# The MLP's first product as seven block products for eight, with weight sums made by adding DMAs

## The chip, the cores and the metric

The kernel runs on one core of a Trainium2 chip. The metric is the device time of one execution in microseconds (us), taken as the median of several runs. One execution of the kernel before was also recorded by the profiler; all rows below are from that one. The engines are called TensorE (PE in the rows; PEld is its weight loading), VectorE (DVE), ScalarE (ACT), GpSimd (POOL) and SyncE (SP).

## What is computed

One layer on a sequence of 512 tokens of width 1024, in float32: a mixer of two branches (retention with 8 heads, and sparse attention with 16), merged by gates; then an MLP; then a gated input from a per-layer embedding; then a last norm. The MLP is the part that the change rewrites:

```
h2 = rms_norm(x, norm_mlp_g)
x = x + square(relu(h2 @ w_mlp_up)) @ w_mlp_down
x = x + (p @ w_ple_proj) * sigmoid(rms_norm(x, norm_ple_g) @ w_ple_gate)
return rms_norm(x, norm_final_g)
```

`w_mlp_up` is 1024 x 4096 and `w_mlp_down` 4096 x 1024. In the retention, every head's output goes through a group norm, `(o - mean) * rsqrt(var + eps)`, over its 256 columns.

## The kernel before

Every product is made of three matmuls in a rounded float32 format: both operands are split into a high part (ScalarE's copy, `hi`) and a low part (VectorE's subtraction, `lo`), and `mm3` adds high by high, low by high and high by low in one PSUM bank. So each weight that comes from memory costs one pass of ScalarE and one of VectorE before TensorE can use it. Activations lie transposed (128 features by 512 tokens), so that a weight block of 128 by 128 is loaded into TensorE and 512 token columns stream past it. The retention's value product and the last product stream 256 columns past a loaded block in places.

The program is a list of items in one order, written by hand. An item has a TensorE part, a step after it (`post`) and the weight parts (512 columns each) that it needs. `run` goes through the list: it splits the item's own parts if they aren't, records its matmuls, splits up to three parts ahead (the fourth one's high part too), records what earlier items deferred, and then the item's `post`. Each engine works through its own instructions strictly in that order. A weight piece (1024 columns, 512 KB) is loaded by a DMA that SyncE issues as soon as one of three buffers (`raw`) is free, that is, when VectorE has made the low part of the second half of the piece three before it; high and low parts have four buffers each.

The stages that matter here: the retention's heads (`head_dense` of head h interleaved with `head_core` of head h-1, about 40 us a head, and after every second head `ret_out`, about 22 us); the attention; the merge and `w_out`, which makes the residual `x1` in eight blocks of 128 features; the MLP in two halves of 2048 hidden units, each `up` (16 products of 24 matmuls) and then `down` (8 products of 48); the embedding's gate product and the delivery of the output.

Around the changed lines: `gained` makes the high and low part of a block of `x1` (`gx`) and adds its squares to `acc1`. `token_rstd` and `over_partitions` make the token norm's factor `rb1`, by which `up`'s step multiplies. `rsqrt` is nine small instructions, on VectorE or, for heads 0 to 6 (`pool if h < NH - 1 else dve`) and for the first two token tiles of the output, on GpSimd. `gated` is the step that makes a head's output ready for `ret_out`. `finish` and `deliver` are the steps of the output's four token tiles; the last tile's second half is computed in two products of 256 columns.

Of the kernel before, what the change touches and what calls it, by code (L numbers as in the profile page):

```python
# [140 lines left out]
def _layer_kernel(ctx, tc, a, out):  # L141
# [35 lines left out]
    def issue(p):  # L177
        if p.keep:
            if p.raw is None:
                p.raw = P_[p.keep].tile([P, p.n], F32, name=f"raw_{p.keep}_{p.mark}")  # L180
                sp.dma_start(p.raw, p.src)
        elif p.raw is None:
# [3 lines left out]
            sp.dma_start(p.raw, p.src)  # L186
# [607 lines left out]
    def head_core(h):  # L794
# [36 lines left out]
        def post():  # L831
# [9 lines left out]
            rs = rsqrt(ve, NQ, "gn", pool if h < NH - 1 else dve)  # L841
# [29 lines left out]
        its.append(Item(0.9, turn, gated))  # L871
# [40 lines left out]
    items += [sil0, g0[0], b0[1], g0[1], c1[3], g0[2], c0[0], g0[3], c1[4], c0[1], qk0[0], c0[2], qk0[1], c0[3], qk0[2], qk0[3], c0[4]]  # L912
    for h in range(1, NH):
        its = mixed(head_dense(h), head_core(h - 1))
# [334 lines left out]
    def merge_start():  # L1249
        close("aw", "q", "kv")  # L1250
        T["nsa_p"] = []
        open_("np", bufs=1)
        open_("mp", bufs=1, side="right")
# [42 lines left out]
    def out_start():  # L1296
        close("mw", "np", "oret")
        xp = open_("xp", bufs=1)
        T["x1"] = [xp.tile([P, S], F32, name=f"x1_{n}") for n in range(KT)]
        T["gx"] = [(xp.tile([P, S], F32R, name=f"gx_hi{n}"), xp.tile([P, S], F32R, name=f"gx_lo{n}")) for n in range(KT)]  # L1300
        T["rb1"] = xp.tile([P, S], F32, name="rb1")
        open_("ew", bufs=2)
# [3 lines left out]
    def gained(n, g, acc):  # L1306

        hi, lo = T["gx"][n]
        x = T["x1"][n]
        gc = gains[:, g + n : g + n + 1]  # L1310
        act.activation(hi, x, AF.Copy, scale=gc)
        dve.scalar_tensor_tensor(lo, x, gc, hi.bitcast(F32), op0=ALU.mult, op1=ALU.subtract)
# [8 lines left out]
    for n in range(KT):  # L1321
# [5 lines left out]
        def post_x(ps, n=n):  # L1327
            dve.tensor_tensor(T["x1"][n], ps, T["xs", n], op=ALU.add)
            gained(n, G_MLP, "acc1")
# [4 lines left out]
    gxs = (lambda: T["gx"], KT)  # L1334
    hid = {}

    def up(hf, i):
        def post(ps):
            t = P_["ew"].tile([P, S], F32, tag="t1", name="relu")
# [289 lines left out]
```

## Time and profile before

| | |
|---|---|
| median of 3 runs | 1269.36 us (1267.52 to 1271.04) |
| the profiled execution's own time | 1269.14 us |
| its span in the trace | 1267.4 us |
| mean granted TensorE clock | 0.997 of full speed |
| TensorE busy | 1245.6 us, 98% of the span |
| VectorE, ScalarE, GpSimd busy | 61%, 42%, 17% |

The profile is read from the busy shares to the waits of the engine that is busy all the time, and from there to single stretches: what a matmul takes there from start to start, and what the other engines have to do in the same stretch. A duration of a row can overlap the next row's by the pipeline of an engine, so spacing is read from starts.

### The profile page before, as it was taken

The page shows a single profiled execution, that of the slowest core. Times are in us where ns is not written, and L with a number is a line of the kernel's source. Part 1 is how long each engine was busy: PE and PEld are TensorE (multiplying, and loading weights), DVE is VectorE, ACT ScalarE, POOL GpSimd, SP SyncE. Part 2 cuts the span into 40 slices and gives each one's busy share as a digit, 9 for nine tenths or more (in the row PEclk, how much of TensorE's full clock was granted, in tenths as well). Part 3 has the DMA queues.
Part 4 walks back from the last instruction along what each step waited for, and adds up shares of the span by engine and source line. Part 5 has one row for each costly group of instructions (what it writes and reads, how often), then busy time and mean ns, then how long its engine had stood idle before and what let it go on. Part 6 is the DMA issues. An engine that isn't in the chain of part 4 may idle for free.

```text
span 1267.4 us, 16784 instructions
## 1 busy us (share of the span) xinstructions
PE 1245.6 (98%) x6312; PEld 1033.0 (82%) x6312; DVE 770.9 (61%) x1401; ACT 528.8 (42%) x1091; POOL 213.4 (17%) x290
## 2 busy tenths in 40 slices
PE   8999999999999999999999999999999999999996
PEld 6968898898998987788888888888888888888885
DVE  6766763665666587778878754555652345644456
ACT  5753333332332233677778642343322223323333
POOL 0040000000000023556574500000000000000045
PEclk9999999999999999999999999999999999999998
DMA  7532323223223222211010033332233342323221
GB/s 248 204 133 67 105 79 100 76 92 100 76 78 98 86 73 84 67 34 35 34 51 17 18 100 100 122 127 91 93 100 100 98 168 86 98 100 100 88 79 67
DMA packets 34513, 116.29 MB, mean 92 GB/s; under 512 B 4096, under 2 KB 4480, under 8 KB 34304
## 3 DMA queue, kind: packets, MB, share of 16 engines
q1 hardware_dynamic: 34432, 115.22, 27.8%
q8 instruction: 50, 0.82, 0.3%
q14 instruction: 31, 0.25, 0.1%
HBM read 111.01 MB, written 4.19 MB: 91 GB/s over the span
## 4 chain that ended last, share of the span: by engine, by line
PE 50%; DVE 2%; POOL 0%; ACT 0%; issue 0%; DVEq 0%; ACTq 0%
PE ps_s L256 6%; PE ps_s L257 6%; PE ps_s L258 6%; PE ps_d L256 4%; PE ps_d L258 4%; PE ps_d L257 4%; PE ps_v L256 3%; PE ps_v L257 3%; PE ps_v L258 3%; PE ps_t L1089 2%; PE ps_t L258 1%; PE ps_t L257 1%; PE ps_t L256 1%; PE ps_v L1106 1%; PE ps_v L1105 1%; PE ps_s L1014 1%
## 5 line engine op out<-in xcount | busy, mean ns | idle before, releaser
L206 ACT ACTIVATE hi<-raw 128x512 fp32r<-128x512 f32 (+1 forms) x364 | 222.7, 622 | 256.4 <-PE ps_v L258 60.5
L209 DVE TENSOR_TENSOR lo<-raw,hi 128x512 fp32r<-128x512 f32 (+1 forms) x350 | 242.5, 715 | 67.7 <-ACT hi L206 67.6
L209 POOL TENSOR_TENSOR lo_fw<-raw_fw,hi_fw 128x512 fp32r<-128x512 f32 x8 | 11.3, 1437 | 503.0 <-ACT hi_fw L206 503.0
L256 PE MATMUL ps_d<-h_hi,hi 128*128 128x512 f32 x216 | 89.6, 415 | 0.0
L258 PE MATMUL ps_d<-h_hi,lo 128*128 128x512 f32 x216 | 85.4, 395 | 0.0
L257 PE MATMUL ps_d<-h_lo,hi 128*128 128x512 f32 x216 | 85.3, 395 | 0.0
L1067 POOL TENSOR_TENSOR pr<-pr,rr 128x512 f32<-128x512 f32 x80 | 84.5, 1087 | 0.0
L1032 ACT ACTIVATE pr<-ps_s,nm 128x128 f32<-128x128 f32 (+3 forms) x128 | 66.0, 525 | 21.5 <-DVE sc L1026 15.5
L256 PE MATMUL ps_t<-h_hi,hi 128*128 128x512 f32 x160 | 64.2, 401 | 0.0
L1098 DVE TENSOR_TENSOR ptl<-ps_t,pth 128x512 fp32r<-128x512 f32 x80 | 53.9, 684 | 16.5 <-ACT pth L1093 14.5
L258 PE MATMUL ps_t<-h_hi,lo 128*128 128x512 f32 x160 | 63.4, 396 | 0.3 <-DVE lo L209 0.3
L257 PE MATMUL ps_t<-h_lo,hi 128*128 128x512 f32 x160 | 63.3, 395 | 0.0
L1024 DVE TENSOR_REDUCE nm<-ps_s 128x2 f32<-128x256 f32 (+3 forms) x64 | 52.1, 815 | 14.3 <-PE ps_s L1017 14.0
L302 POOL TENSOR_TENSOR rs_q<-rs_y 128x4 f32<-128x4 f32 (+1 forms) x9 | 4.4, 491 | 325.9 <-DVE rs_y L292 325.9
L1343 ACT ACTIVATE hh<-relu 128x512 fp32r<-128x512 f32 x32 | 20.3, 634 | 93.5 <-DVE relu L1340 93.5
L1093 ACT ACTIVATE pth<-ps_t 128x512 fp32r<-128x512 f32 x80 | 47.3, 598 | 22.6 <-PE ps_t L1089 18.6
L258 PE MATMUL ps_s<-hh,lo 128*128 128x512 f32 x128 | 50.8, 397 | 0.0
L256 PE MATMUL ps_s<-hh,hi 128*128 128x512 f32 x128 | 50.7, 396 | 0.0
L257 PE MATMUL ps_s<-hl,hi 128*128 128x512 f32 x128 | 50.7, 396 | 0.0
L256 PE MATMUL ps_s<-gx_hi,hi 128*128 128x512 f32 x128 | 50.6, 395 | 0.0
L258 PE MATMUL ps_s<-gx_hi,lo 128*128 128x512 f32 x128 | 50.5, 395 | 0.0
L257 PE MATMUL ps_s<-gx_lo,hi 128*128 128x512 f32 x128 | 50.5, 395 | 0.0
(459 smaller groups left out, 3388.4 us busy)
## 6 DMA issues: line engine op xcount, KB each, us to landing
raw<-in_w_ret_qkg_dram SPq DMA_DIRECT2D x32, 512.0 KB, 3.4
raw<-in_w_mlp_up_dram SPq DMA_DIRECT2D x32, 512.0 KB, 3.7
raw<-in_w_mlp_down_dram SPq DMA_DIRECT2D x32, 512.0 KB, 3.6
raw<-in_w_ret_v_dram SPq DMA_DIRECT2D x16, 512.0 KB, 3.5
raw<-in_w_ret_o_dram SPq DMA_DIRECT2D x16, 512.0 KB, 3.5
raw<-in_w_merge_gate_dram SPq DMA_DIRECT2D x16, 512.0 KB, 3.6
raw<-in_w_nsa_dram SPq DMA_DIRECT2D x12, 512.0 KB, 3.5
o_ret<-in_cmp_w_dram SPq DMA_DIRECT2D x8, 512.0 KB, 5.1
```

What stands on the lines that cost most here:

```text
L206: act.activation(p.hi[i], p.raw[:, c], AF.Copy)
L209: eng.tensor_tensor(p.lo[i], p.raw[:, c], p.hi[i].bitcast(F32), op=ALU.subtract)
L256: pe.matmul(ps, sh, mh, start=first, stop=False)
L257: pe.matmul(ps, sh, ml, start=False, stop=False)
L258: pe.matmul(ps, sl, mh, start=False, stop=last)
L1024: dve.tensor_reduce(self.nm[:, j, :], self.seen(j), axis=AX.XY, op=ALU.max, negate=True)
L1032: act.activation(self.pr[:, j, br, 0 : self.nk].rearrange("p (b j) -> p b j", j=P), self.seen(j)[:, br], AF.Exp, bias=self.nm[:, j, br : b ...
L1067: pool.tensor_tensor(p, p, self.rr[:, :, 1 + br : 2 + br].broadcast_to([P, 4, P]), op=ALU.mult)
L1089: pe.transpose(self.t[i][:, j * P : (j + 1) * P], self.pr[:, j, br, kb * P : (kb + 1) * P], ident)
L1093: act.activation(hi, self.t[i], AF.Copy)
L1098: dve.tensor_tensor(lo, self.t[i], self.pt[i][0].bitcast(F32), op=ALU.subtract)
L1343: act.activation(hi, t, AF.Square)
```

## The change

**The product.** Per pair q of output blocks (16 pairs) the weights are four blocks `w[i][j]` (i: which 512 input features, j: which 128 outputs) and the activations four blocks (512 features by 256 tokens). Where eight products of blocks did the work, seven do now, on sums and differences of blocks (the scheme of Strassen and Winograd). Four of the seven use a sum of weights, `s1` to `s4`; all stream 256 token columns. Partial results are taken out of PSUM in between, since three banks per pair are each used for more than one of the products. The token factor is no longer multiplied into `up`'s result; its square (`rb2`) is multiplied into `down`'s.

**The weight sums** are made in device memory by 32 plain copies that ScalarE issues and 32 adding DMAs that GpSimd issues, 512 KB each, spread by `among` over heads 1 to 6. MLP weights then come in 56 pieces of two DMAs of 256 KB each, where they came in 32 pieces of 512 KB.

**The activations' sums** (`combined`, in `w_out`'s stage): VectorE makes the difference `t1` and GpSimd three more, each of 128 by 256.

**Around it.** `rsqrt` is on VectorE everywhere; the last head's `gated` is recorded ahead of the splits; `w_out`'s step defers `gained`; the output's steps come in another order, the last product's gain is multiplied on VectorE, and ScalarE issues one of the last two stores.

```diff
@@ Piece
+    def load(self, sp):
+        if isinstance(self.src, list):
+            for i, x in enumerate(self.src):
+                w = self.n // len(self.src)
+                sp.dma_start(self.raw[:, i * w : (i + 1) * w], x)
...
@@ _layer_kernel
+    w_up = a["w_mlp_up"].rearrange("(q i) k (j c) -> i j q k c", i=2, j=2)
+    sums = {x: dram.tile([16, P, S], F32, name=f"sum_{x}") for x in ("s1", "s2", "s3", "s4")}
+    def sum_steps():
+        todo = {}
+        for c in range(8):
+            q = slice(2 * c, 2 * c + 2)
+            w = lambda i, j, q=q: w_up[i, j, q]
+            t = {x: v[q] for x, v in sums.items()}
+            levels = [("s1", w(1, 1)), ("s3", w(0, 0)), ("s2", w(0, 0)), ("s4", w(0, 1))], [("s1", w(1, 0)), ("s3", w(1, 0))], [("s2", t["s1"])], [("s4", t["s2"])]
+            for l, level in enumerate(levels):
+                todo.setdefault(c + l, []).extend((t[x].rearrange("q k c -> k q c"), src.rearrange("q k c -> k q c"), l > 0) for x, src in level)
+        return [lambda d=d, s_=s_, add_=add_: pool.dma_start(d, s_, accum_op=ALU.add, max_dma_last_dim=4 * S) if add_ else act.dma_start(d, s_) for n in sorted(todo) for d, s_, add_ in todo[n]]
...
-            rs = rsqrt(ve, NQ, "gn", pool if h < NH - 1 else dve)
+            rs = rsqrt(ve, NQ, "gn")
...
-        its.append(Item(0.9, turn, gated))
+        its.append(Item(0.9, turn, gated, eager=h == NH - 1))
...
     for h in range(1, NH):
-        its = mixed(head_dense(h), head_core(h - 1))
+        its = among(mixed(head_dense(h), head_core(h - 1)), folds_[64 * (h - 1) // 6 : 64 * h // 6])
...
+    def combined(n, g):
...
+        taken("x10", k, t[:, :H])
+        taken("x11", k, t[:, H:])
+        pool.tensor_tensor(d, d, t[:, H:], op=ALU.add)
+        pool.tensor_tensor(t0[:, H:], t[:, H:], t0[:, H:], op=ALU.subtract)
+        pool.tensor_tensor(t0[:, :H], d, t[:, :H], op=ALU.subtract)
+        def rest():
+            taken("t2", k, d, -1.0)
+            taken("t3", k, t0[:, H:])
+            taken("t4", k, t0[:, :H])
+        defer(rest)
...
             dve.tensor_tensor(T["x1"][n], ps, T["xs", n], op=ALU.add)
-            gained(n, G_MLP, "acc1")
+            defer(lambda: gained(n, G_MLP, "acc1", True))
...
+    class UpPair:
+        def product(self, name, piece, col):
+            ps_, x, first = {"p5": ("b", "t1", True), "m1": ("a", "x00", True), "m2": ("c", "x10", True), "p6": ("a", "t2", False), "p3": ("b", "x11", False),
+                             "p7": ("a", "t3", False), "p4": ("a", "t4", False)}[name]
+            def go():
+                if first:
+                    tag = {"a": "dv"[self.q % 2], "b": "t", "c": "s"}[ps_]
+                    setattr(self, ps_, bank(tag, (P, H)))
+                ps = getattr(self, ps_)
+                for k in range(4):
+                    mm3(ps, *piece.cols(col + k * P, col + k * P + P), *seventh(x, k), first and k == 0, k == 3, not first)
...
+        def squares(self, i, t):
...
+            dve.scalar_tensor_tensor(t, t, 0.0, t, op0=ALU.min if i else ALU.max, op1=ALU.mult)
+            act.activation(hi, t, AF.Copy)
+            defer(lambda: dve.tensor_tensor(lo, t, hi.bitcast(F32), op=ALU.subtract))
...
+        order_ = [("p5", 0), ("m1", 0), ("p5", 1), ("m1", 1), ("m2", 0)]
+        for i in range(6):
+            order_ += [("p6", i)] + [("m1", i + 1)] * (i > 0) + [("p3", i), ("p7", i), ("p5", i + 2), ("m2", i + 1), ("p4", i)]
...
     def down(hf, n):
-            dve.tensor_tensor(x, ps, x, op=ALU.add)
+            t = P_["ew"].tile([P, S], F32, tag="t1", name="dn")
+            dve.tensor_tensor(t, ps, T["rb2"], op=ALU.mult)
+            dve.tensor_tensor(x, x, t, op=ALU.add)
...
-            st["r"] = rsqrt(v, 1, "fn", pool if t < NQ - 2 else dve)
+            st["r"] = rsqrt(v, 1, "fn")
...
+            behind.extend([gate_, *scaled, held, take, square] if t == NQ - 1 else [gate_, take, *scaled, square])
```

On ScalarE, in the middle of head 1 (`th`, `inh`, `vh` and `rth` are steps of the head, `hi` a weight's high part), the order before is:

```order
L206 ACTIVATE hi<-raw 128x512 x2
L754 ACTIVATE th<-ps_v 128x512
L316 ACTIVATE inh<-inn 128x256
L316 ACTIVATE inh<-inn 128x128
L206 ACTIVATE hi<-raw 128x512 x4
L764 ACTIVATE vh<-ps_d 128x512
L764 ACTIVATE vh<-ps_v 128x512
L867 ACTIVATE rth<-gated 128x512 x2
```

and after it is as follows, with the copies of weight sums (`sum_s`) among the same instructions:

```order
L214 ACTIVATE hi<-raw 128x512 x2
L780 ACTIVATE th<-ps_v 128x512
L360 DMA sum_s_81<-in_w_mlp_up_dram 128x2x512
L324 ACTIVATE inh<-inn 128x256
L324 ACTIVATE inh<-inn 128x128
L360 DMA sum_s_83<-in_w_mlp_up_dram 128x2x512
L214 ACTIVATE hi<-raw 128x512 x4
L790 ACTIVATE vh<-ps_d 128x512
L790 ACTIVATE vh<-ps_v 128x512
L360 DMA sum_s_80<-in_w_mlp_up_dram 128x2x512
L893 ACTIVATE rth<-gated 128x512 x2
```

Nothing else moved there: five or six copies a head stand between the head's own steps.

On VectorE, in the middle of `up`, two output blocks of the kernel before (`relu` is the step's result, `hl` its low part, `lo` a weight's low part) are:

```order
L1340 SCALAR_TENSOR_TENSOR relu<-ps_s,rb_8181 128x512
L1344 TENSOR_TENSOR relu<-relu 128x512
L1345 TENSOR_TENSOR hl<-relu,hh 128x512
L209 TENSOR_TENSOR lo<-raw,hi 128x512 x2
L1340 SCALAR_TENSOR_TENSOR relu<-ps_d,rb_8181 128x512
L1344 TENSOR_TENSOR relu<-relu 128x512
L1345 TENSOR_TENSOR hl<-relu,hh 128x512
L209 TENSOR_TENSOR lo<-raw,hi 128x512 x2
```

and one pair (seven products) after it is, from the step after `m2` to the next pair's (`r` are the two results of a pair, `s` the partial results that ScalarE took out of PSUM):

```order
L1467 TENSOR_TENSOR r_9209<-ps_s,s_9125 128x256
L217 TENSOR_TENSOR lo<-raw,hi 128x512
L1481 COPY r_9168<-ps_d 128x256
L1489 SCALAR_TENSOR_TENSOR r_9168<-r_9168 128x512
L217 TENSOR_TENSOR lo<-raw,hi 128x512
L1491 TENSOR_TENSOR hl<-r_9168,hh 128x512
L217 TENSOR_TENSOR lo<-raw,hi 128x512 x2
L1473 TENSOR_TENSOR r_9209<-ps_t,s_9125 128x256
L1489 SCALAR_TENSOR_TENSOR r_9209<-r_9209 128x512
L217 TENSOR_TENSOR lo<-raw,hi 128x512
L1491 TENSOR_TENSOR hl<-r_9209,hh 128x512
L1478 TENSOR_TENSOR r_9313<-ps_v,s_9036 128x256
```

With the two `lo` that follow, a pair has seven low parts of weights where it had four, four steps of 256 columns that read PSUM, and two squares with their low parts.

## Rows read from the trace of the kernel before

**Rows 1.** The page: busy time and share by engine; tenths in 40 slices.
```profile
PE 1245.6 (98%) x6312; PEld 1033.0 (82%) x6312; DVE 770.9 (61%) x1401; ACT 528.8 (42%) x1091; POOL 213.4 (17%) x290
PEclk9999999999999999999999999999999999999998
```
**Rows 2.** Waits of TensorE: line, waited for, us in total, times, longest.
```profile
PE ps_d L256 <- ACT hi L206: 5.8, 1, 5.8
PE ps_d L257 <- DVE rtl L868: 1.0, 2, 0.7
PE ps_d L256 <- ACT rth L867: 0.3, 1, 0.3
```
**Rows 3.** Timeline of TensorE (start, duration): first matmuls of second `up`, second `down`.
```profile
1026.87 0.39 PE L256 MATMUL ps_d<-gx_hi,hi 128*128 128x512 f32 x1
...
1116.47 0.40 PE L256 MATMUL ps_d<-hh,hi 128*128 128x512 f32 x1
```
**Rows 4.** Stretches: us, busy (x) of PE, PEld, DVE, ACT, POOL, clock, DMA share, GB/s.
```profile
95.00:390.00 295.00, 295.00 (x1690) 257.35 (x1689) 180.97 (x350) 97.32 (x180) 15.71 (x66) 1.00 0.28 86
1027.00:1116.00 89.00, 89.00 (x383) 71.58 (x382) 51.06 (x78) 27.94 (x47) 0.00 (x0) 1.00 0.32 111
1249.94:1255.55 5.61, 5.61 (x49) 5.60 (x47) 4.26 (x11) 2.99 (x7) 4.09 (x10) 1.00 0.26 96
```
**Rows 5.** Timeline of TensorE's weight loading in `up`.
```profile
929.93 0.19 PEld L257 LDWEIGHTS ps_s<-gx_lo,hi 128*128 128x128 f32 x1
```
**Rows 6.** Timeline of VectorE in the first `up`.
```profile
900.79 1.28 DVE L209 TENSOR_TENSOR lo<-raw,hi 128x512 fp32r<-128x512 f32 x2
903.64 0.69 DVE L1340 SCALAR_TENSOR_TENSOR relu<-ps_v,rb 128x512 f32<-128x512 f32 x1 [1.56 <-PE ps_v L258]
905.03 0.69 DVE L1344 TENSOR_TENSOR relu<-relu 128x512 f32<-128x512 f32 x1 [0.70 <-ACT hh L1343]
905.75 0.69 DVE L1345 TENSOR_TENSOR hl<-relu,hh 128x512 fp32r<-128x512 f32 x1
```
**Rows 7.** Groups by line and form: busy us, mean ns of one.
```profile
L814 DVE TENSOR_TENSOR inn<-ps_t,dec 128x256 f32<-128x256 f32 x8 | 3.3, 417 | 0.0
L537 ACT ACTIVATE vcat<-ps_v 128x256 fp32r<-128x256 f32 x1 | 0.4, 385 | 0.0
L206 ACT ACTIVATE hi<-raw 128x512 fp32r<-128x512 f32 x356 | 219.5, 626 | 256.4 <-PE ps_v L258 60.5 <-PE ps_d L257 53.4 <-PE ps_s L257 52.9
L1432 POOL TENSOR_TENSOR x2t<-x2t,gf 128x256 f32<-128x256 f32 x2 | 1.8, 902 | 0.0
```
**Rows 8.** DMA queue (packets, MB, share of 16 engines); issues (KB each, us to landing).
```profile
q1 hardware_dynamic: 34432, 115.22, 27.8%
raw<-in_w_mlp_up_dram SPq DMA_DIRECT2D x32, 512.0 KB, 3.7
xs<-in_xT_dram SPq DMA_DIRECT2D x8, 256.0 KB, 4.0
```
**Rows 9.** Timeline of the issuing queue in the heads: one issue, one decay table.
```profile
230.31 0.33 SPq L186 DMA_DIRECT2D raw<-in_w_ret_qkg_dram  x1
230.69 0.42 SPq L781 DMA_DIRECT2D dec<-in_decay_dram  x1
```
**Rows 10.** VectorE's wait for the group norm's factors: us, times, longest.
```profile
DVE on L846 <- POOL rs_y L298: 21.0, 7, 3.0
```
**Rows 11.** Timeline at the end: GpSimd beside VectorE, last matmul, last scaling.
```profile
1245.92 1.29 POOL L1432 TENSOR_TENSOR x2t<-x2t,gf 128x512 f32<-128x512 f32 x1 [3.61 <-ACT sq L1431]
1245.99 1.77 DVE L1427 TENSOR_TENSOR x2t<-x2t,pth 128x512 f32<-128x512 f32 x1
1255.48 0.28 PE L258 MATMUL ps_s<-hi_fw,gx_lo 128*128 128x256 f32 x1
1260.38 0.14 DVE L1443 TENSOR_SCALAR fv<-ss 128x1 f32<-128x1 f32 x1
1263.08 0.72 ACT L1451 ACTIVATE o<-x2t,rs_y 128x512 f32<-128x512 f32 x1 [3.22 <-DVE rs_y L300]
```

More of the change, by code (lines that the diff above doesn't have):

```diff
@@ L1313, in gained @@
+    def gained(n, g, acc, seven=False):
+        x = T["x1"][n]
+        if seven:
+            combined(n, g)
+        else:
+            hi, lo = T["gx"][n]
+            gc = gains[:, g + n : g + n + 1]
+            act.activation(hi, x, AF.Copy, scale=gc)
+            dve.scalar_tensor_tensor(lo, x, gc, hi.bitcast(F32), op0=ALU.mult, op1=ALU.subtract)
         if n == 0:
@@ L1390, in ple_start @@
+    dn = [down(1, n) for n in range(KT)]
+    items += dn[0] + [Item(0, load_pp)] + sum(dn[1:], [])
     def ple_start():
         close("hid")
-        open_("fw", bufs=1, side="right")
+        open_("fw", bufs=1)
         for p in w_pg[1]:
@@ L1482, in _layer_kernel @@
     items += weave(first[16:], turns[4:])
-    behind, late, last = [], [], [(), ()]
-    def finished(steps, ends=(), turn=True):
-        gate_, take, square = steps
-        behind.extend([gate_, *late[:1], take, *(last.pop(0) if turn else ()), *late[1:]])
-        late[:] = [square, *ends[:1]]
-        last.append(ends[1:])
+    behind = []
+    f_ = [finish(t, 0, S, lambda t=t: pw[0, t], 0) for t in range(NQ)]
+    behind.append(f_[0][0])
     for t in range(NQ):
-        finished(finish(t, 0, S, lambda t=t: pw[0, t], 0))
+        behind.extend([*(f_[t + 1][:1] if t + 1 < NQ else ()), *f_[t][1:]])
     banks = iter("ttdvs")
+    scaled = []
     for t in range(NQ):
@@ L1510, in _layer_kernel @@
                         add(Item(0, None, behind.pop(0)))
-            ends = deliver(t, 2 + (t == NQ - 1)) if c1 == S else ()
-            finished(finish(t, S + c0, S + c1, lambda t=t, c0=c0, n=c1 - c0: pw[1, t, c0][:, :n], 1 + (c0 > 0)), ends, t < NQ - 1 or c0 > 0)
-    items += [Item(0, None, f) for f in [*behind, late[0], *last[0], late[1], *last[2]]]
+            gate_, take, square = finish(t, S + c0, S + c1, lambda t=t, c0=c0, n=c1 - c0: pw[1, t, c0][:, :n], 1 + (c0 > 0), c0 == 0)
+            if t == NQ - 1 and c0 == 0:
+                behind.extend([gate_, take])
+                held = square
+                continue
+            behind.extend([gate_, *scaled, held, take, square] if t == NQ - 1 else [gate_, take, *scaled, square])
+            factors, last_ = deliver(t, 2 + (t == NQ - 1))
+            behind.append(factors)
+            scaled = [last_]
+    items += [Item(0, None, f) for f in [*behind, *scaled]]
     run(items)
```

198 lines of the change are left out of this document (138 added, 60 removed).

## The prediction, made before the changed kernel ran

> **What bounds the kernel now.** I read the busy shares first: TensorE works 1245.6 of 1267.4 us and no other engine passes 61%, at the full granted clock in every slice but the last [rows 1]. The waits of TensorE come next: of its 21.8 us without work, 5.8 are the first weights at the start, about 1.3 are waits for a head's output (`rth`, `rtl`) [rows 2], and 11.9 lie behind the last matmul, which starts at 1255.48 [rows 11]. So time goes away only with TensorE's work, its few waits, or the tail. The second `up` shows it at its plainest: 384 matmuls of 512 columns from 1026.87 to 1116.47 [rows 3], 0.2333 us from start to start, TensorE busy for 89.00 of 89 us [rows 4]. The sum is made against the profiled execution's own time, 1269.14 us: its span of 1267.4 and 1.7 around it. That is the median of the runs shown (1269.36) to 0.02%.
>
> **The product.** Out go 2 x 384 = 768 matmuls at 0.2333: 179.2 us. In come 16 pairs x 7 products x 4 blocks x 3 = 1344 matmuls of 256 columns. Their price stands in the last stretch of the trace, where 48 matmuls of this form take 5.61 us [rows 4]: 0.1169 each, half of the wide ones to within 0.2%. 1344 x 0.1169 = 157.1 us. **Saved: 22.1 us**, if TensorE is fed.
>
> One thing speaks against that half. In the 256-column stretch weight loading is busy for 5.60 of 5.61 us, in `up` for 71.58 of 89 [rows 4]; there is no room left behind the matmuls for a slower load. The Trainium skill (TensorE: Matmul & The Clock Gate, Back-to-back issue gap) has the spacing set by the load and the matmul together, 81 ns at 128 columns and 131 at 512, so that half the columns are not half the time: about 0.75 of it at 256, my estimate on a straight line between its figures, by which the product would cost 235 us and the sum below would end 78 us higher, near 1326. The measured half decides.
>
> **Feeding it.** A pair takes TensorE 84 x 0.1169 = 9.8 us. VectorE has seven `lo`, two squares, two `hl` and four steps of 256 columns in that time. Two 512-wide instructions that don't need each other start 0.60 apart (a pair of 0.69 takes 1.28); one that needs the one before starts 0.72 after it [rows 6]; a 256-wide one takes 0.42 [rows 7]. 11 x 0.60 + 4 x 0.42 = 8.3 us, 85%. I walked one period in the order that stands in the code, from the end of `p4`: copy and square done at 1.3, `lo`, `hl` (its high part comes back from ScalarE 1.4 after the square's start, as from 903.64 to 905.03 in rows 6) at 2.7, two `lo` at 3.9, then a wait for `p3` (4.2), two more steps, `lo`, `hl` at 6.9, the step after `p7` at 7.2, two `lo` at 8.4, the step after `m2` at 9.0, `lo` at 9.6, and a wait for the next `p4`. Each `lo` is there 2 to 3 us ahead of its product, and each bank is empty before its next use. ScalarE has 7 x 0.63 + 3 x 0.39 + 2 x 0.63 = 6.8 us. Loads: two of 256 KB every 2.8 us, 187 GB/s; the queue moved 115.22 MB in 27.8% of the span, so at full work about 327 GB/s, and a 256 KB load lands in 4.0 us [rows 8]. A buffer comes free two pieces (5.6 us) before VectorE wants the new data; issue 0.33 [rows 9], landing 4.0 and ScalarE's 0.63 leave 0.6, and then the 2 to 3 us above. So nothing waits in the steady part. Both halves begin and end less evenly (`p4` of the last pair comes one product behind `p7`, whose step waits behind a `lo` and an `hl`): I take **+1.5** for both, between 0 and 13 (the rival below).
>
> **The sums of weights.** 64 DMAs of 512 KB are spread over six stretches of 40 us, 10.7 in each, beside loads that take 0.28 of the DMA engines [rows 4], or 11 us. No row shows a copy from memory to memory or an adding one. At 327 GB/s a copy is 1.6 us of all engines and an add lies between 1.6 and 4.8 (three passes): 17 to 34 us, in all 28 to 45 of 40. I take two passes for an add, 36 of 40. A load is needed every 5.6 us with a cover of two pieces less its landing of 3.7 [rows 8], 11.2 - 3.7 = 7.5 us; if three queues share the engines evenly, 1.6 us of data become 4.8 and the load lands 3.2 later. It is hidden; if that cover went, each late load would cost its excess. ScalarE issues 32 copies at 0.33 to 0.42 [rows 9], 13 us in 240 where it is a third busy; what is queued behind one (a `hi`, a bank's emptying) comes half a microsecond later, against parts made three ahead. Its waits are for DMAs that lie eight back, some 16 us. GpSimd has nothing else to do there. **+1**, between 0 and 8.
>
> **The group norm's factors.** VectorE waits 3.0 us a head for GpSimd's chain [rows 10]; its own takes 9 x 0.2 = 1.8. TensorE waits for neither: **0**, bounds -0.5 and +1. **The last head's `gated` ahead of the splits** takes away the waits on `rth` and `rtl`: **-1**, bounds -1.3 and 0.
>
> **From `w_out` to `up`.** For blocks 4 to 7 VectorE has two `lo`, the addition, the squares' sum and five low parts of 256 in each 5.6 us: 4.6. GpSimd's three steps (0.90 each [rows 7]) run beside them, and beside GpSimd a VectorE instruction of 0.69 took 1.77 [rows 11]; 2.7 us of that cost VectorE about 1.6, in all 6.2 of 5.6. It falls 2.4 us behind over four blocks, with three parts of 2.8 us in hand. The first product that needs GpSimd's sums, `p6`, stands five products (7 us) behind the last matmul of `w_out`; the chain (addition, gain, GpSimd, high, low) with the `lo` between is 7 to 8.5 us long against 8.05 for its last block. **+1**, bounds 0 and +3. `down`'s added multiplication is 16 x 0.69 on a VectorE that has 11.2 us per product: 0.
>
> **The tail.** Behind the last matmul stand gate, product, square, factors and scaling: today the last scaling starts 7.6 us behind it, and 2.7 of them are the factors (1260.38 to 1263.08) [rows 11]. The new order puts the last tile's steps ahead of less: by the rows' durations scaling begins at about 5.7 to 6.4. **-1.5**, bounds -2.5 and +0.5.
>
> **Sum:** 1269.1 - 22.1 + 1.5 + 1 - 1 + 1 - 1.5 = **1248.0 us**.
>
> **The rivals.**
> - *VectorE or the loads set the pace of `up`.* By whole durations VectorE has 4.80 + 2.77 + 1.67 = 9.2 us a pair; if `hl` finds nothing to do while its high part is made, 0.7 comes twice, 10.6 of 9.8: 16 x 0.8 = 13 us, **1260**. Against it: the walk finds a `lo` to fill each such gap. For it: VectorE works strictly in order, and a load that lands 1 us late shifts all behind it.
> - *Loads of the heads land late.* If an add costs three passes, the DMA engines are asked for 45 of 40 us, and the excess, 5 us x 6, is only partly caught by the `ret_out` stretches between: about 9 us, **1257**.
> - *The adds can't keep up: slower than before.* They stand in one queue, ahead of GpSimd's steps for the attention's queries. 32 adds have about 340 us, from 105 to 445, 10.6 us each. Up to there a slow add costs nothing; beyond, each microsecond costs 32 us, and 11.5 us an add gives 1248 + 29 = **1277**. Against it: a load of the same bytes lands in 3.7 us. For it: each add waits for the DMA before it, read and write of the same memory, and no row has one. The Trainium skill (DMA: Bandwidth & Descriptors, Issuing engines are not separate DMA queues) says that DMAs of the three queues share the same 16 engines; no row here shows that.
> - *The narrow matmuls don't run at half price:* a weight load of 0.19 [rows 5] that nothing hides makes 1344 x 0.19 = 255 us, **1346**, slower. The stretch of 48 speaks against it; it is short, which is all that speaks for it. The Trainium skill's rule above (TensorE: Matmul & The Clock Gate, Back-to-back issue gap) is of this kind.
>
> **How the numbers follow.** My forecast, within 1243 to 1253: 0.62. `up` paced by VectorE or loads, 1253 to 1265: 0.17. Late loads in the heads, 1253 to 1266: 0.12. Adds that block GpSimd: 0.07. Narrow matmuls at a higher price: 0.02. The likeliest is 1248. The range reaches from the lower bounds (1243: all of the tail and the waits gained) into both middle rivals up to 1262. A measurement can tell 0.3% (3.8 us) from no change. Faster by more than that, under 1265.6: 0.62 + 0.17 + 0.11, less 0.02 for what I overlooked, 0.88; within: that 0.02 and 0.01 of the late loads, 0.03; slower: 0.07 + 0.02 = 0.09.
>
> **What would show it.** In the changed profile: the two `up` stretches at 78 to 80 us each with TensorE busy throughout (right), or at 85 with waits on `lo` (the first rival); the six head stretches still without a TensorE wait, DMA share near 0.9; adding DMAs landing in under 10 us; the step from `w_out` to `up` with a wait under 3 us; the last store some 10 us behind the last matmul. Wrong is the prediction if matmuls of 256 columns lie more than 0.12 apart where nothing waits, if a wait on the sums stands in the critical chain, or if `hi` in the heads waits for DMAs.

## The result, and the profile of the changed kernel

The changed kernel takes **1251.78 us** (median of 4 runs, 1250.18 to 1252.07) against 1269.46 for the kernel before beside it: 0.9859 of the time, 95% interval 0.9842 to 0.9876. Forecast were 1248.0, within 1243 to 1262. The direction, the range and the mechanism hold; of the 21.1 us of the forecast's sum 17.1 came in the profiled execution (1252.07 us, span 1250.2). In the experiments below four executions took 2.4 to 6.9 ms; they are left out of every median.

The page answers to [rows 1 and 8]; adds stand in queue q0, copies of weights in q10, and the last number of an issue is its time to landing:

```profile
PE 1227.0 (98%) x6888; PEld 1047.8 (84%) x6888; DVE 835.9 (67%) x1594; ACT 579.1 (46%) x1215; POOL 237.3 (19%) x234
...
q1 hardware_dynamic: 46816, 127.54, 30.9%
q0 software_dynamic: 8704, 16.78, 8.0%
q10 hardware_dynamic: 8848, 17.04, 4.1%
...
sum_s<-in_w_mlp_up_dram ACTq DMA_DIRECT2D x32, 512.0 KB, 5.7
...
sum_s<-in_w_mlp_up_dram POOLq DMA_DIRECT2D x16, 512.0 KB, 7.8
sum_s<-sum_s POOLq DMA_DIRECT2D x16, 512.0 KB, 12.4
```

TensorE's waits (line, waited for, us in total, times, longest), to be read beside [rows 2]:

```profile
PE ps_d L264 <- ACT hi L214: 5.8, 1, 5.8
PE ps_v L266 <- DVE lo L217: 1.7, 2, 1.2
PE ps_t L369 <- DVE acc L494: 1.1, 1, 1.1
...
PE ps_d L265 <- DVE rtl L894: 1.0, 2, 0.7
PE ps_v L264 <- DVE r L1478: 0.4, 2, 0.2
...
PE ps_d L264 <- ACT rth L893: 0.3, 1, 0.3
PE ps_d L264 <- DVE o_ret L913: 0.2, 1, 0.2
```

No wait on a sum of weights is among them. The waits on `rth` and `rtl`, which the early `gated` was to remove, stand there with the same 1.3 us. TensorE's busy time fell by 18.6 us, not by the 22.1 of the product.

Where the time went shows best when both traces are cut at the same matmuls: the first of 304 columns (the first projections' end), the last on `rth` or `rtl` (the heads' end), the first of each `up` and `down`, the first on `w_ple_gate`, the last of all. These are five of the cuts in the changed kernel (TensorE's timeline: start, duration), as in [rows 3]:

```profile
25.06 0.30 PE L264 MATMUL ps_d<-hi,h_hi 128*128 128x304 f32 x1
...
847.50 0.28 PE L264 MATMUL ps_t<-gt,hi 128*128 128x256 f32 x1
...
930.96 0.40 PE L264 MATMUL ps_d<-hh,hi 128*128 128x512 f32 x1
...
1020.57 0.28 PE L264 MATMUL ps_t<-gt,hi 128*128 128x256 f32 x1
...
1100.55 0.39 PE L264 MATMUL ps_d<-hh,hi 128*128 128x512 f32 x1
```

| stretch, us | before | after | difference | forecast |
|---|---|---|---|---|
| start, to the first 304-column matmul | 23.55 | 25.06 | +1.5 | 0 |
| heads, to the last on `rth`, `rtl` | 482.92 | 483.84 | +0.9 | 0 (sums +1, `gated` -1, factors 0) |
| merge and `w_out`, to the first `up` | 339.40 | 338.60 | -0.8 | 0 |
| first `up` | 91.04 | 83.46 | -7.6 | -9.3 (-11.05, transition +1, half of the feeding +0.75) |
| first `down` | 89.96 | 89.61 | -0.35 | 0 |
| second `up` | 89.60 | 79.98 | -9.6 | -10.3 (-11.05, +0.75) |
| second `down` | 89.96 | 89.60 | -0.36 | 0 |
| `w_ple_gate`, to the last matmul | 49.05 | 49.11 | +0.1 | 0 |
| tail | 11.92 | 10.94 | -1.0 | -1.5 |

The last column sums to -21.1 and the measured differences to -17.2. Six entries are off the forecast by half a microsecond or more: the start, the heads, the merge, the two `up` and the tail. The merge ranges from 338.5 to 339.5 us over the eleven profiles with the new product, so its 0.8 tells little. The experiments take up the others; each is read by the same cuts, which tell tenths of a microsecond where the whole time tells one or two.

### The profile page after: what moved, and what is told of

Read it like the earlier page. It is cut to its first block, busy times and chain, and to the rows that moved or that the text cites. A ratio compares the mean times of both kernels' runs of the same rounds, so it can differ in the third digit from the quotient of the medians.

```text
span 1250.2 us, 18607 instructions
## 1 busy us (share of the span) xinstructions
PE 1227.0 (98%) x6888; PEld 1047.8 (84%) x6888; DVE 835.9 (67%) x1594; ACT 579.1 (46%) x1215; POOL 237.3 (19%) x234
## 3 DMA queue, kind: packets, MB, share of 16 engines
q0 software_dynamic: 8704, 16.78, 8.0%
q10 hardware_dynamic: 8848, 17.04, 4.1%
## 4 chain that ended last, share of the span: by engine, by line
PE 46%; DVE 5%; ACT 1%; issue 1%; DVEq 0%; ACTq 0%
PE ps_s L266 4%; PE ps_s L264 4%; PE ps_s L265 4%; PE ps_d L266 4%; PE ps_d L265 4%; PE ps_d L264 4%; PE ps_v L264 3%; PE ps_v L266 3%; PE ps_v L265 3%; PE ps_t L265 2%; PE ps_t L266 2%; PE ps_t L264 2%; PE ps_t L1127 2%; PE ps_v L1144 1%; PE ps_v L1143 1%; PE ps_s L1052 1%
## 5 line engine op out<-in xcount | busy, mean ns | idle before, releaser
L214 ACT ACTIVATE hi<-raw 128x512 fp32r<-128x512 f32 (+1 forms) x412 | 250.4, 622 | 238.0 <-PE ps_s L265 54.8
L217 DVE TENSOR_TENSOR lo<-raw,hi 128x512 fp32r<-128x512 f32 (+1 forms) x398 | 279.4, 717 | 58.7 <-ACT hi L214 58.4
L264 PE MATMUL ps_d<-h_hi,hi 128*128 128x512 f32 x216 | 89.6, 415 | 0.0
L360 POOL DMA_DIRECT2D sum_s<-in_w_mlp_up_dram x16 | 18.3, 1147 | 222.8 <-DMA sum_s<-in_w_mlp_up_dram 222.8
L266 PEld LDWEIGHTS ps_d<-h_hi,lo 128*128 128x128 f32 x216 | 40.6, 188 | 10.0 <-DVE lo L217 0.3
L1127 PEld LDWEIGHTS ps_t<-cst,pr 128*128 128x128 f32 x320 | 39.3, 140 | 10.7 <-issue 1.6
L1127 PE MATMUL ps_t<-cst,pr 128*128 128x128 f32 x320 | 48.0, 273 | 0.0
L264 PEld LDWEIGHTS ps_d<-h_hi,hi 128*128 128x128 f32 x216 | 40.7, 188 | 7.0 <-ACT tanh L433 0.4
## 6 DMA issues: line engine op xcount, KB each, us to landing
sum_s<-sum_s POOLq DMA_DIRECT2D x16, 512.0 KB, 12.4
```

What stands on the lines that cost most here:

```text
L214: act.activation(p.hi[i], p.raw[:, c], AF.Copy)
L217: eng.tensor_tensor(p.lo[i], p.raw[:, c], p.hi[i].bitcast(F32), op=ALU.subtract)
L264: pe.matmul(ps, sh, mh, start=first, stop=False, skip_group_check=again)
L266: pe.matmul(ps, sl, mh, start=False, stop=last, skip_group_check=again)
L360: return [lambda d=d, s_=s_, add_=add_: pool.dma_start(d, s_, accum_op=ALU.add, max_dma_last_dim=4 * S) if add_ else act.dma_start(d, s_) ...
L1127: pe.transpose(self.t[i][:, j * P : (j + 1) * P], self.pr[:, j, br, kb * P : (kb + 1) * P], ident)
```

## The experiments

Eleven runs follow, one of them of the changed kernel as it is. Times are medians where a kernel ran more than once; the kernel before beside them took 1269.3 to 1269.7.

**1. What 256 columns cost.** The kernel before, with `up` in halves:

```diff
-    for p, c, k in mine:
-        mm3(st["ps"], *p.cols(c, c + P), *x[k], k == 0, k == nk - 1)
+    for cut in ((slice(0, S // 2), slice(S // 2, S)) if halves else (slice(0, S),)):
+        for p, c, k in mine:
+            mm3(st["ps"][:, cut], *p.cols(c, c + P), *(v[:, cut] for v in x[k]), k == 0, k == nk - 1, halves)
...
```

> The kernel before, with every product of w_mlp_up computed as two halves of 256 columns: 1536 matmuls of 256 in place of 768 of 512, the same multiplications, nothing else changed. Theory (a 256-column matmul in this place costs 0.1183 us from start to start, as the second `up` of the changed kernel shows, and not the 0.1169 that the prediction took from the last stretch): each `up` takes 768 x 0.1183 = 90.9 us for 89.6, together +2.5, so 1272.0 us. Rival 1 (half of the wide price, 0.1169): +0.2 an `up`, 1269.9. Rival 2 (a weight load of 0.19 that is not hidden): 146 us an `up`, 1382. Beside that its start is read: if the 1.5 us that the changed kernel loses before 25 us belong to the change, the first 304-column matmul starts here at 23.5 us as before; if they are a matter of when the clock rises, it may start at either.

1273.77 us, 1.0037 of before (1.0024 to 1.0050). The two halves of a product begin their sums in one bank, and what comes out is not the layer's result; number, shape and order of the matmuls are those described. Its second `up` on TensorE's timeline, from its first matmul to the first of `down`:

```profile
1029.35 0.27 PE L256 MATMUL ps_d<-gx_hi,hi 128*128 128x256 f32 x1
...
1120.48 0.39 PE L256 MATMUL ps_d<-hh,hi 128*128 128x512 f32 x1
```

91.13 us for 768 matmuls: **0.1187** each, with nothing new in the kernel but the width. Weight loading is busy all the time there (columns as in [rows 4]):

```profile
1030.00:1120.00 90.00, 90.00 (x760) 90.00 (x760) 50.66 (x78) 27.46 (x46) 0.00 (x0) 1.00 0.31 107
```

In the changed kernel the second `up` has 672 in 79.98 us, of which 0.46 are one wait for `r` and the slow matmul behind it: 0.1183. The theory holds for this stretch, and the prediction's price was too low. It is not one price, though. The first `up` of the same kernel takes 93.88 us, 2.8 more than before where 1.3 were expected, and TensorE waits for nothing in it. Behind the squares' sum and the factors that lie in it, 649 matmuls of 256 columns stand between these two starts:

```profile
861.51 0.29 PE L258 MATMUL ps_s<-gx_hi,lo 128*128 128x256 f32 x1
...
939.39 0.39 PE L256 MATMUL ps_d<-hh,hi 128*128 128x512 f32 x1
```

That is 0.1200 each, at the full granted clock. What makes the same matmuls 0.0013 us slower there than in the second `up` stays open. A price nearer than the prediction's stood in the trace of before all along, in the heads, where 126 matmuls of 256 columns lie between these two rows of TensorE's timeline of the kernel before:

```profile
118.42 0.34 PE L256 MATMUL ps_d<-hi,h_hi 128*128 128x256 f32 x1
...
133.36 0.27 PE L857 MATMUL ps_s<-cst,on 128*128 128x128 f32 x1
```

14.94 us for 126: 0.1186, or 0.1182 without the first, which takes 0.17. And the stretch that the prediction did use was misread: its window of 5.61 us closes 0.07 us behind the start of the 48th matmul [rows 4, 11], so 5.61 is 47 distances and a piece of one. From the first start to the last, 47 distances in 5.54 us, it says 0.1179.

**2. What the sums of weights cost.** No DMAs for them; the four products that need them read plain blocks:

```diff
-    folds_ = sum_steps()
+    folds_ = []
...
-            self.w = {"m1": w_up[0, 0, q], "m2": w_up[0, 1, q], "p4": w_up[1, 1, q], "p5": sums["s1"][q], "p6": sums["s2"][q], "p7": sums["s3"][q], "p3": sums["s4"][q]}
+            self.w = {"m1": w_up[0, 0, q], "m2": w_up[0, 1, q], "p4": w_up[1, 1, q], "p5": w_up[1, 0, q], "p6": w_up[1, 0, q], "p7": w_up[0, 0, q], "p3": w_up[0, 1, q]}
```

> The changed kernel without the 64 DMAs that sum the weights; the products p3, p5, p6 and p7 read plain blocks of w_mlp_up in their place, so what it computes is not the reference's. Theory (the DMAs cost the heads about 0.9 us and `up` nothing): the stretch from the first 304-column matmul to the last on rth shortens by 0.5 to 0.9, both `up` stay at 83.5 and 80.0 us, 1251.0 us. Rival 1 (the DMAs cost nothing, the 0.9 come from the factors on VectorE): all stretches as in the changed kernel, 1251.8. Rival 2 (what `up` loses over 1344 matmuls at half price comes from reading the sums): each `up` shortens by 1 to 1.5, 1249.

1251.18 us. From the first matmul on `rth` to the last the heads take 321.89 us, with the sums 321.87; both `up` take 83.45 and 79.98. My theory falls, rival 1 holds: the 64 DMAs cost nothing. The same stretch of the heads with them and without (the columns are those of [rows 4]), first the changed kernel:

```profile
250.00:300.00 50.00, 50.00 (x286) 43.60 (x285) 35.35 (x72) 16.46 (x29) 8.03 (x7) 1.00 0.87 227
```

and the kernel without sums:

```profile
250.00:300.00 50.00, 50.00 (x286) 43.58 (x286) 34.47 (x71) 16.37 (x30) 0.00 (x0) 1.00 0.29 88
```

The DMA engines go from 0.29 to 0.87 of their time, TensorE works 50.00 of 50 us in both.

**3. Where the DMA engines run out.** Every sum a second time, into tensors that nothing reads:

```diff
+    sums_b = {x: dram.tile([16, P, S], F32, name=f"sumb_{x}") for x in ("s1", "s2", "s3", "s4")}
-    t = {x: v[q] for x, v in sums.items()}
+    for sums_ in (sums, sums_b):
+        t = {x: v[q] for x, v in sums_.items()}
...
-    folds_[64 * (h - 1) // 6 : 64 * h // 6]
+    folds_[128 * (h - 1) // 6 : 128 * h // 6]
```

> The changed kernel with every sum of weights made twice, the second time into tensors that nothing reads: 128 DMAs in place of 64, in the same six stretches. Theory of the prediction (the DMA engines' shares add up, and a late load costs TensorE its excess): the heads' share of 0.28 before and 0.76 now goes to 1.24 of what there is, 24% of 270 us do not fit, loads come late and TensorE loses 10 to 60 us there, 1262 to 1310. Rival (loads keep their share and the sums only finish later; nothing waits for them until 830 us): DMA share near 1 in the heads and after, the adds trail beyond 400 us, TensorE loses under 2 us, 1252 to 1254. The run without the sums took nothing off the heads, which speaks for the rival at the single amount.

**1268.76 us** (1266.67 to 1274.86; the profiled execution took 1272.91), 0.9995 of before (0.9979 to 1.0011): the whole gain of the change is gone. Both `up` and both `down` take what they took; from the first 304-column matmul to the first on `rth` it is 7.7 us longer, from there to the heads' end 13.2. Three stretches of its heads:

```profile
150.00:200.00 50.00, 45.22 (x253) 38.52 (x252) 30.00 (x63) 14.98 (x28) 10.29 (x9) 0.93 1.08 295
200.00:250.00 50.00, 50.00 (x287) 43.56 (x286) 23.41 (x53) 18.59 (x33) 9.16 (x8) 1.00 1.07 290
300.00:350.00 50.00, 45.81 (x211) 36.85 (x212) 26.26 (x44) 14.69 (x26) 9.16 (x8) 0.97 1.09 280
```

and its waits of TensorE between 100 and 450 us:

```profile
PE ps_t L264 <- ACT hi L214: 6.1, 2, 4.4
PE ps_t L266 <- DVE lo L217: 3.0, 1, 3.0
PE ps_t L264 <- DVE inn L842: 2.0, 1, 2.0
PE ps_d L264 <- DVE o_ret L915: 0.6, 1, 0.6
PE ps_d L264 <- ACT hi L214: 0.5, 1, 0.5
```

The share stands at 1.07 to 1.09 in these stretches, with 280 to 295 GB/s, and everything lands later: a load of `w_ret_qkg` in 7.5 us for 4.3, a copy of a sum in 17.4 to 26.0 for 5.7. So loads do land late, as the prediction's rival "loads of the heads land late" had it. But they are the smaller part of what holds `hi`. ScalarE's waits between 100 and 450 us:

```profile
ACT hi L214 <- DMA sum_s<-in_w_mlp_up_dram: 26.1, 6, 9.7
...
ACT hi L214 <- DMA sumb_s<-in_w_mlp_up_dram: 11.4, 4, 5.0
ACT hi L214 <- DMA raw<-in_w_ret_o_dram: 11.4, 5, 4.4
ACT hi L214 <- issue: 10.9, 6, 5.1
...
ACT hi L214 <- DMA raw<-in_w_ret_qkg_dram: 8.6, 6, 2.8
```

By the releases that the profile names, 37.5 us lie behind copies that ScalarE issued itself and 20.0 behind loads; in the changed kernel none lies behind a copy and 3.2 behind loads. (Behind "issue" stands no release that the profile shows.) TensorE's longest wait, 4.4 us at 303, is of the first kind:

```profile
292.11 10.27 ACTq L362 DMA_DIRECT2D sumb_s<-in_w_mlp_up_dram  x2
302.42 0.63 ACT L214 ACTIVATE hi<-raw 128x512 fp32r<-128x512 f32 x1 [9.69 <-DMA sum_s<-in_w_mlp_up_dram]
```

Between its two issues ScalarE stood until an earlier copy had landed, and the `hi` came right behind. The load that this `hi` reads was not the reason: it was issued at 287.73 us or before (the next one is issued at 297.37), and loads of that stretch land within 8.4 us. The prediction had named these waits ("for DMAs that lie eight back, some 16 us") and taken them as covered; with copies that land in 17.4 to 26.0 us they are not. How much each of the two costs was not separated by a run.

TensorE's 12.2 us of waits cost 20.9, for the most part because the clock falls behind them: in the stretches with a wait the granted clock is 0.93 and 0.97, in the one without it 1.00, and behind the wait at 303 matmuls of 512 columns lie 0.43 us apart at a granted clock of 0.50 (304.4 to 307.0 us). The share alone does not decide: between 200 and 250 us it is 1.07 as well, and TensorE waits for nothing. The Trainium skill (DMA: Bandwidth & Descriptors, Issuing engines are not separate DMA queues) has all queues share the same 16 engines; the later landing of SyncE's loads beside DMAs that ScalarE and GpSimd issued agrees with that.

**4. The group norm's factors back on GpSimd.**

```diff
-    rs = rsqrt(ve, NQ, "gn")
+    rs = rsqrt(ve, NQ, "gn", pool if h < NH - 1 else dve)
```

> The changed kernel with the group norm's factors back on GpSimd (heads 0 to 6), as before. Theory (the part priced at 0 is what makes the sums possible: on GpSimd the factors would stand in the queue behind adding DMAs that wait 8 to 18 us each for the DMA before them): `on` waits up to 10 us a head in place of the 3.0 of before, TensorE waits behind it, +10 to +60 us, 1262 to 1310. Rival (the adds leave gaps in GpSimd's queue, so that the factors pass as before): 1252 within 1 us.

1251.09 us. The theory falls: VectorE waits for the factors 20.9 us in 7 waits, as in [rows 10]; adding DMAs do not stand in their way. The heads are even 0.5 us shorter (321.39; five profiles with the factors on VectorE and the full clock say 321.87 to 321.91). So this part of the change is neither needed by the sums nor of use: it costs about half a microsecond. The other 0.4 of the heads' 0.9 stand at one place: in the last `ret_out` TensorE waits 0.2 us for `o_ret` and has a slow matmul behind it, which the kernel before has not. It stays with the factors on GpSimd; what makes `o_ret` late was not tried.

**5. `gated` of the last head behind the splits again.**

```diff
-    its.append(Item(0.9, turn, gated, eager=h == NH - 1))
+    its.append(Item(0.9, turn, gated))
```

> The changed kernel with the last head's `gated` behind the splits again, as before. Theory (rth stands on ScalarE behind two copies into qcat that wait for GpSimd until 484.1 us, so calling `gated` earlier gains nothing): the waits on rth, rtl and o_ret stay at 1.2 to 1.5 us in all, the stretch between the first matmul on rth and the first of w_mlp_up the same within 0.4 us. Rival (the early `gated` took away its 1 us and something else put it back): the waits grow by about 1 us, to 2.5.

One execution, 1251.32 us; the waits on `rth` and `rtl` are the same 0.3 and 1.0. The heads' length is 322.99 us, 1.1 more, which looks like the gain of the early call. The unaltered kernel, run again, shows that it is not:

> The changed kernel once more, unaltered, to read what differs from one execution to the next. Theory (the start differs by when the clock rises and when the first loads land): the first 304-column matmul starts anywhere from 22.8 to 25.4 us, the stages behind it as in the first profile within 0.5 us each; 1251 to 1252 us. Rival (the 1.5 us of the first profile belong to the change): it starts at 25 us again.

1251.39 us; its heads take 323.00 us, with the early call in place, 1.1 more than in the first profile where 0.5 at most was expected. Behind the wait on `rtl` its matmuls lie 0.43 us apart, in the first profile 0.23 (TensorE's timeline of the repetition):

```profile
487.98 0.50 PE L265 MATMUL ps_d<-rtl,hi 128*128 128x512 f32 x1 [0.74 <-DVE rtl L894]
...
489.07 0.63 PE L265 MATMUL ps_v<-rtl,hi 128*128 128x512 f32 x1
489.50 0.63 PE L266 MATMUL ps_v<-rth,lo 128*128 128x512 f32 x1
```

In the same stretch its granted clock was 0.50 (the lower level, 1.2 GHz), that of the first profile 1.00. First the repetition, then the first profile:

```profile
488.50:491.00 2.50, 2.50 (x7) 1.92 (x7) 2.50 (x6) 0.00 (x0) 0.51 (x1) 0.50 0.52 154
```

```profile
488.50:491.00 2.50, 2.46 (x11) 2.02 (x12) 2.50 (x6) 0.00 (x0) 0.00 (x0) 1.00 0.36 52
```

So after the same waits the clock falls in some executions and not in others, and that is worth 1.1 us here. It fell (0.50) in the run without the early call too, and between the two with the fallen clock, 322.99 and 323.00, the early call does nothing: on ScalarE `rth` stands behind two copies into `qcat`, which wait for GpSimd until 484.1 us, and starts at 485.4 us however early it is called.

**The start**, by the way, is the same kind of difference. The first 304-column matmul starts at 23.55 and 23.23 in the two profiles with the old product, and at 25.06, 24.24, 24.75, 25.15, 24.13, 25.35, 23.39, 22.77, 24.50, 24.61 and 23.54 in the eleven with the new one, none of which alters anything there. In the first profile TensorE caught up with VectorE (the wait of 1.1 on `acc`), and from 17.0 to 20.5 us it had a granted clock of 0.52; in the repetition no wait and 1.00. The mean of the eleven is 24.3, that of the two 23.4. Of the table's 1.5 us some 0.7 are therefore one execution's lot; with a spread of 2.6 us and only two profiles on one side, whether the rest belongs to the change stays open.

**6. How much room VectorE has in `up`.** Additions of 512 columns that write a tile nothing reads, two a pair, then four:

```diff
     def after_m2(self):
         ...
+        dve.tensor_tensor(T["junk"], T["x1"][0], T["x1"][1], op=ALU.add)
```

> The changed kernel with two further additions of 512 columns a pair on VectorE in both `up` (behind the steps of m2 and p7; they write a tile that nothing reads). VectorE is busy for 56.56 of 65 us in the second `up`, 1.27 us a pair are free, and two additions take 1.2. Theory (the walk of the prediction: about 8.4 of 9.9 us a pair, each gap can be filled): `up` loses at most 0.3 us a pair, 80 to 85 us each, 1252 to 1262. Rival (order costs VectorE a whole step a pair, 10.6 of 9.8 us already, hidden by the splits made ahead): +0.7 to 1.2 us a pair, 1263 to 1271.

> The same with four further additions a pair (also behind the steps of m1 and p6): 2.4 us into 1.27 that are free. Theory: VectorE sets the pace at 10.8 us a pair for 9.9, 87 to 89 us an `up`, +14 to +18 us, 1266 to 1270. Rival (as for two): +1.9 to 2.4 us a pair, 1282 to 1290.

1253.43 us and **1267.98 us**. With two the `up` take 84.62 and 80.57 us (+1.2, +0.6), with four 91.98 and 87.40 (+8.5, +7.4). Both times come out as the walk of the prediction had it, neither as the rival; only the first `up` with four lies over the 87 to 89 us expected. The second `up` between 1030 and 1095 us in the changed kernel, then with four additions:

```profile
1030.00:1095.00 65.00, 65.00 (x551) 65.00 (x550) 56.56 (x99) 38.51 (x79) 0.00 (x0) 1.00 0.58 187
```

```profile
1030.00:1095.00 65.00, 63.05 (x511) 61.09 (x511) 62.12 (x111) 34.73 (x72) 0.00 (x0) 1.00 0.52 166
```

VectorE is busy for 87% in the changed kernel; the 1.27 us a pair that it has free take two additions of 0.6, and of the further 1.2 nearly all shows: 1.13 x 16 = 18 us were expected, 15.9 came.

**7. From `w_out` to `up`.** The three sums of activations of blocks 4 to 7 on VectorE:

```diff
-    pool.tensor_tensor(d, d, t[:, H:], op=ALU.add)
+    dve.tensor_tensor(d, d, t[:, H:], op=ALU.add)
```

(and the two lines behind it in the same way)

> The changed kernel with the three sums of activations of blocks 4 to 7 on VectorE in place of GpSimd. Theory (GpSimd beside VectorE stretches VectorE's instructions, 0.69 to 1.23 and 0.75 for two to 1.30, and that is why it falls behind from w_out to `up`): the three cost 3 x 0.34 = 1.0 us a block and give back about 2, the waits on lo at 852 to 856 us (1.3) go, the first `up` takes 82.2 for 83.5 us, 1250.5 us. Rival (VectorE has 4.6 us of work in 5.6 and cannot take 1.0 to 1.3 more): the waits grow to about 3 us, 1253.5.

1251.0 and 1251.3 us. The first `up` takes 82.54 us for 83.46, so most of the 1.3 expected. VectorE's timeline in the changed kernel, while GpSimd does the sums:

```profile
843.82 1.30 DVE L1364 TENSOR_TENSOR gt<-gf,gt 128x256 fp32r<-128x256 f32 x2
845.04 1.23 DVE L1417 TENSOR_TENSOR acc<-acc,sq 128x512 f32<-128x512 f32 x1
846.19 1.22 DVE L217 TENSOR_TENSOR lo<-raw,hi 128x512 fp32r<-128x512 f32 x1
```

GpSimd's third sum, beside the last of them:

```profile
845.68 1.18 POOL L1392 TENSOR_TENSOR gf<-gd,gf 128x256 f32<-128x256 f32 x1
```

and the same instructions where VectorE does them itself:

```profile
844.17 0.75 DVE L1364 TENSOR_TENSOR gt<-gf,gt 128x256 fp32r<-128x256 f32 x2
844.84 0.42 DVE L1390 TENSOR_TENSOR gd<-gd,gf 128x256 f32<-128x256 f32 x1
845.18 0.42 DVE L1391 TENSOR_TENSOR gf<-gf,gf 128x256 f32<-128x256 f32 x1
845.51 0.42 DVE L1392 TENSOR_TENSOR gf<-gd,gf 128x256 f32<-128x256 f32 x1
845.85 0.69 DVE L1417 TENSOR_TENSOR acc<-acc,sq 128x512 f32<-128x512 f32 x1
846.45 0.69 DVE L217 TENSOR_TENSOR lo<-raw,hi 128x512 fp32r<-128x512 f32 x1
```

Three instructions of 0.34 apart are added, and each of the others gets 0.54 back: what GpSimd took off VectorE cost VectorE more than it saved. The Trainium skill (SBUF — State Buffer, Terms) has the two engines share a pair of ports that one of them holds for a whole instruction while the other waits; 1.23 beside GpSimd and 0.69 without agree with that.

**8. The last head and the tail.** `rth` of the last head on VectorE, its low part right behind it; in the tail no step for GpSimd and both last stores from SyncE:

```diff
-    act.activation(hi, t, AF.Copy, scale=0.5)
...
+    dve.tensor_scalar_mul(hi, t, 0.5)
...
-    ... 1 + (c0 > 0), c0 == 0)
+    ... 1 + (c0 > 0), t < NQ - 1)
...
-    (act if cols == 3 else sp).dma_start(out[rows, 0:S], o[:, 0:S])
+    sp.dma_start(out[rows, 0:S], o[:, 0:S])
...
-    dve.tensor_scalar_mul(o[:, S:c], x2(t, S, c), r[:, 0:1])
-    dve.scalar_tensor_tensor(o[:, c:], x2(t, c, D), r[:, 0:1], T["gf"][:, c:], op0=ALU.mult, op1=ALU.mult)
+    dve.scalar_tensor_tensor(o[:, S:], x2(t, S, D), r[:, 0:1], T["gf"][:, S:], op0=ALU.mult, op1=ALU.mult)
```

> The changed kernel with two places altered. Last head: the high parts rth come from VectorE, right behind `gated`, with their low parts. Tail: the last tile's second half gets its gain in the one scaling step on VectorE and GpSimd has nothing to do there; both last stores go through SyncE. Theory: the waits on rth and rtl (1.2 us) go, since VectorE has both by 485 us and TensorE comes at 485.8; of the tail 0.5 go with GpSimd's step beside VectorE (0.92 for 0.42) and up to 0.4 with the store from ScalarE's queue (2.8 us to landing against 2.0), 10.0 to 10.3 us behind the last matmul for 10.5 to 11.0; 1250 us. Rival: VectorE is late by what it does in ScalarE's place, the wait comes back at a `lo`, and two stores on one queue land one after the other; 1251.5 to 1252.

One execution, 1251.09 us. For the last head the theory falls, only 0.3 us are gained: the wait on the second `rtl` stays, 1.2 us, because GpSimd works beside VectorE there as well (1.64 us for a step of 0.69). In the tail the last scaling starts 5.5 us behind the last matmul, in the changed kernel 6.05 (1245.31 - 1239.26), in the kernel before 7.60 [rows 11]; from there to the end it is 4.9 us either way. So the order of the tail gained what was forecast, 1.55 us, and 0.57 of it were lost behind it, where before needed 4.32 us. The store from ScalarE's queue is not the reason: from SyncE the end comes no sooner.

**9. All of them together** (experiments 4, 7 and 8):

> The changed kernel with the two alterations of a_ends, the three sums of activations on VectorE and the group norm's factors of heads 0 to 6 on GpSimd. Theory (they touch different stretches and add up): 1.2 in the last head, 0.9 from w_out to `up`, 0.6 in the tail, 0.5 in the heads, 3.2 in all: 1248.5 us, 1.017 times faster than before. Rival (what one place gives, the clock or a later wait takes back): 1250 to 1251.5.

1249.65 us (1248.22 to 1250.86), 0.9852 of before (0.9835 to 0.9868), beside 1251.39 for the changed kernel (0.9864, 0.9849 to 0.9879). The cuts add up as they did singly (heads 321.13, first `up` 82.57, tail 10.35, about 2.2 us for the 3.2 expected, since the last head gives 0.3 and not 1.2); in the whole time the two intervals overlap, so a gain over the changed kernel is not shown by it.

## Why the prediction was right, and where its 4 us went

- **The product** (forecast -22.1): right in its mechanism, mis-sized in its price. 1344 x 0.1183 = 159.0 in place of 157.1: **1.9 us less**. The step that failed is the unit price from a window of 48 matmuls that was cut too short, where a stretch of 126 stood in the same trace.
- **Weight loads that nothing hides** (the rival at 1346, and the rule of the Trainium skill, TensorE: Matmul & The Clock Gate, Back-to-back issue gap, by which half the columns take 0.75 of the time, an estimate): the measured share is 0.1187 of 0.2333, 0.51. The rule does not hold here, though weight loading was busy for all of the 90 us.
- **Feeding** (+1.5): 0.46 us at the end of each `up`, where `p4` of the last pair comes one product behind `p7`, the place that was named. The walk of VectorE stands, by experiment 6: 1.27 us a pair to spare. It was 87% busy for 85% forecast.
- **From `w_out` to `up`** (+1): the first `up` is 3.48 us longer than the second; in the kernel before, the squares' sum that lies in it made 1.44. So 2.0 us, inside the bounds. GpSimd beside VectorE was rightly named as the cause and taken too low; 0.9 of it goes when GpSimd does nothing there.
- **The sums** (+1): 0. Two passes for an add were right: the adds take 8.0% of the engines for 16.78 MB, the copies 4.1% for 17.04. The six pieces of 50 us from 100 to 400 us ran at 0.64 to 0.87, 0.77 in the mean, for 0.9 forecast. An add from the weights lands in 7.8 us and one from the sums in 12.4, 10.1 in the mean, hardly under the 10.6 from which the rival "the adds can't keep up" was to decide. That rival's rule was wrong, not only its chance: it took adds one after another, and several are on their way at a time (two are issued within 2.8 us from 368.7). So the last one is issued at 381 us, and GpSimd's first step for the queries comes at 463.
- **`gated` ahead** (-1): 0. The step that failed is that the call's place decided; ScalarE's queue did.
- **The factors** (0): +0.5, inside the bounds, and against the direction in which the change moves them. The other 0.4 of the heads, the wait on `o_ret`, no term had.
- **The tail** (-1.5): -1.0; the part that was argued came whole, what stands behind the last scaling, the stores' landing included, took 0.57 back, and why was not shown.
- **Not forecast**: +1.5 at the start, -0.8 in the merge and -0.7 in the two `down`. Start and merge differ that much between profiles of kernels with the new product. The `down` do not: 89.96 us in both kernels with the old product, 89.6 in all eleven with the new, though the same matmuls stand in them. Why was not tried.

Product 1.9, start 1.5, transition 1.0, `gated` 1.0, heads otherwise 0.9 and tail 0.5 against the forecast; sums 1.0, feeding 0.6 and the stretches not touched 1.5 for it: 3.7 of the 4.1 us between 1248.0 and 1252.07. The rest is 0.1 outside the span and rounding. That the total is off by 4.1 and not by 6.8 is luck: 3.1 us of errors ran the other way. Two of the prediction's signs did not come either: the first `up` took 83.46 us and not 78 to 80, and the adds of sums land in 12.4 us and not in under 10.

## What to carry to other kernels

Take a unit price from the longest stretch that has it, from first start to first start of what comes next: a window's length over the instructions in it is off by a piece of one, and over 1344 instructions that piece was 2 us. Where one instruction has several prices (0.1179 to 0.1200 here), say so in the range. DMA work on the side was free here at shares of 0.64 to 0.87; twice as much took back the whole gain, and ScalarE, which issued the copies, stood behind them longer than behind late loads. So count the share in the busiest stretch and not over the span, and ask what the issuing engine has to do next. Before an instruction is called earlier, look at what stands in front of it on the engine that executes it.

## What the runs showed of the hardware that I had not expected

- A wait of TensorE costs more than its length when the clock falls behind it: 12.2 us of waits cost 20.9 (experiment 3). Behind the same waits on `rtl` it fell in one execution (0.50 for 2.5 us) and not in another (1.00).
- An adding DMA from memory to memory takes about twice the engine time of a copy a byte (8.0% for 16.78 MB, 4.1% for 17.04).
- The DMA engines' mean share goes to 1.09 in this view, with 280 to 295 GB/s for this mix of loads, copies and adds; the prediction had put full work at 327 from a share over the whole span. The first loads of the changed kernel moved 408 GB/s at 1.02 (10 to 12 us), so full work has no one rate.
- Issuing a copy takes ScalarE 0.56 to 0.69 us in the changed kernel and up to 5.63 us where twice as many are under way (experiment 3).
- 256 columns take 0.1179 to 0.1200 us where 512 take 0.2333: 1 to 3% above half, and 0.1200 and 0.1187 in the two `up` of one kernel (experiment 1). What sets that excess stays open.
